# S5 input stage: products of the turned weights tied to the next half's transposes

## Chip, cores and metric

The kernel runs on one core of one Trainium2 chip. The metric is the time of one launch in device microseconds (us), the median of several runs. TensorE (PE) does matmuls and transposes, ScalarE (ACT) and VectorE (DVE) work element by element and empty PSUM, GpSimd (POOL) and SyncE (SP) here mostly issue DMAs. Each engine executes its own list of instructions in a fixed order; semaphores make one engine wait for another.

## The reference

One layer of an encoder, batch 1, 512 tokens, width 1024: a wide input projection feeds an S5 state-space branch and a gated MLP branch; both are merged by gates, followed by cross-attention to 256 memory tokens and a SwiGLU FFN. What matters here is the S5 branch:

```python
lam_bar = jnp.exp(lam * step)
b_bar = ((lam_bar - 1.0) / lam)[..., None] * b
bu = jnp.einsum('gpc,lbgc->lbgp', b_bar, u.astype(jnp.complex64))
...
_, states = lax.associative_scan(_linear_recurrence, (a, bu), axis=0, reverse=reverse)
...
return jnp.einsum('gcp,lbgp->lbgc', c, states).real
```

There are 32 groups of 16 channels with 64 complex states each, and two directions.

## The kernel before

The large projections run as three products of float32r halves (`whi`, `wlo`) for float32 accuracy. For each block of weights a DMA brings `wraw`, ScalarE casts it to `whi` (line 85), VectorE subtracts to get `wlo` (line 86), and TensorE multiplies (line 358; tiles `pt` in token form, `pf` in feature form). Their PSUM banks come from a pool of five. The S5 branch runs as side work in between: a Python generator (`s5_program`) emits its VectorE work when `tick` grants it time, and `later(n, fn)` puts a function that emits the next step some ticks ahead. A scheduler then sets the order on each engine from the program's dependencies and its own estimate of times, so that the order in which the code emits instructions is not the order of execution, except where `in_order` pins an instruction behind the one emitted just before it on its engine.

The scan works on chunks of 8 positions. The input stage `s5_inputs(o)` makes each chunk's contribution to the state, for four octets `o` of 8 groups and two halves `i` (real and imaginary part):

- VectorE forms the weights `e` in three steps of 128x1024 elements (lines 885, 887 and 889, into `wsx`; a slot of `wsx` is reused by the next octet's same half).
- `turn(i, e)` transposes them on TensorE, eight 128x128 transposes in two groups of four (line 864), each group into one PSUM bank `pw`; ScalarE copies each bank to `wt` (line 865).
- `apply(i, wt)` multiplies by `u`, eight products of 64 columns (line 871; two records each in the trace), into a bank `pz`; `keep` has ScalarE copy it into `zh` in two parts (lines 876 and 877).

The banks `pw` and `pz` come from the pool of three auxiliary banks, given out in the order in which the code asks for them: `aux` returns the next of the three, and the first instruction that writes it waits until the bank's last reader is done. `wt` has two buffers. When all eight halves are in `zh`, VectorE runs the scan (62 steps, from line 898), and the outputs follow much later (`py`, lines 922 to 924).

Around this stage the main stream runs the last part of the projection to `zv` (`pt`, emptied by the gelu of line 975) and the gate projection (`pf`, emptied by the sigmoid of line 1047). ScalarE also has the layer norm of `zt` here: centring (line 1008), squares (line 486) and scaling (line 1014, with the root from POOL, line 1013). Behind the stage come `mixing_setup` (`pws`, `pgb`, `prs`; lines 1027 to 1036) and the spatial mixing (`psv`, line 1063).

Of the kernel before, what the change touches and what calls it, by code (L numbers as in the profile page):

```python
# [41 lines left out]
NO = 4  # L42
GO = G // NO
# [9 lines left out]
def hybrid_layer_kernel(  # L53
# [8 lines left out]
    nc = tc.nc  # L62
# [14 lines left out]
    def bank(name):  # L77
        return pm.tile([P, 512], F32, tag="mm", name=name)

    def aux(name, shape=(P, 512)):  # L80
        return pa.tile(list(shape), F32, tag="aux", name=name)
# [11 lines left out]
    in_order = tc.keep_in_program_order  # L93
# [349 lines left out]
    def later(n, fn):  # L443

        side["later"].append((side["now"] + n, fn))
# [30 lines left out]
    ident = cp.tile([P, P], F32, name="ident")  # L476
# [139 lines left out]
    st = {}  # L616
# [150 lines left out]
    def inner(t, gs, n):  # L767

        return t[:, gs, :].unsqueeze(3).to_broadcast([P, GO, t.shape[2], n])

    def outer(t, gs, n):

        return t[:, gs, :].unsqueeze(2).to_broadcast([P, GO, n, t.shape[2]])

    def lc(t, g):
        return t[:, g].rearrange("p a b -> p (a b)")
# [72 lines left out]
    turned = set()  # L849

    def s5_inputs(o):

        gs = slice(o * GO, (o + 1) * GO)
        br, bi = st["b"]
        pr, pi = st["pw"]
        zh, u = st["zh"], st["u"]

        def turn(i, e):
            turned.add((o, i))
            wt = s5p.tile([P, GO, P], F32, tag="wt", name="wt", bufs=2)  # L860
            for hf in range(2):
                ps = aux("pw", (P, 4, P))
                for j in range(4):
                    nc.tensor.transpose(ps[:, j, :], lc(e, 4 * hf + j), ident)
                nc.scalar.copy(wt[:, 4 * hf:4 * hf + 4, :], ps)
            later(0.5, lambda: apply(i, wt))

        def apply(i, wt):
            ps = aux("pz", (P, GO, NCH))
            for g in range(GO):  # L870
                nc.tensor.matmul(ps[:, g, :], wt[:, g, :], u[:, o * GO + g, :], start=True, stop=True)  # L871
            zv = zh[:, :, i, gs].rearrange("p n g -> p g n")
            later(0.5, lambda: keep(zv, ps))

        def keep(zv, ps):
            nc.scalar.copy(zv[lo_], ps[lo_])
            nc.scalar.copy(zv[hi_], ps[hi_, :, ::-1])
            st["nz"] = st.get("nz", 0) + 1

        for i in range(2):  # L880
            while o > 0 and (o - 1, i) not in turned:
                yield None
            e = wsx[:, 2 + i].rearrange("p g (c l) -> p g c l", c=C)
            w = s5p.tile([P, GO, C, Q], F32, tag="etmp", name="etmp2")
            V.tensor_tensor(e, inner(br, gs, Q), outer((pr, pi)[i], gs, C), ALU.mult)
            yield 1.1
            V.tensor_tensor(w, inner(bi, gs, Q), outer((pi, pr)[i], gs, C), ALU.mult)
            yield 1.1
            V.tensor_tensor(e, e, w, (ALU.subtract, ALU.add)[i])
            yield 1.1  # L890
            later(1, lambda i=i, e=e: turn(i, e))
# [93 lines left out]
    u = s5p.tile([P, G, NCH], F32, tag="u", name="u")  # L985
# [74 lines left out]
    for h in range(H):  # L1060
        ps = bank("psv")
# [425 lines left out]
    for t0 in (0, 2):  # L1487
        ps = {t: bank(f"pt{t - t0}") for t in (t0, t0 + 1)}
# [77 lines left out]
    ps = [bank("pf0"), bank("pf1")]  # L1566
# [242 lines left out]
```

## Time and profile before

| | |
|---|---|
| median of 3 runs | 893.77 us (893.14 to 894.84) |
| span of the profiled execution | 891.3 us |
| the stage's transposes and products on TensorE | 83.2 to 151.7 us |
| TensorE busy in the span | 881.1 us |

The profile is of one execution, and the page gives its span (first to last instruction) but no launch time of its own; the runs' times include what lies before and after the span. A row of the chain of waits or of the order of time gives a start, a duration, the engine, the line and the tile written. In the order of time a bracket at the end is idle time of the engine before the row and what ended it. In the windows' answer each row is a stretch, then busy time and number of instructions of PE, its weight loads, DVE, ACT and POOL, the granted clock as a share of full speed, and the DMA load.

### The profile page before, as it was taken

Reading aid. Unit: us, or ns where it says so; the run is one execution under the profiler, and the core shown is the slowest. Engines: PE = TensorE matmul, PEld = TensorE weight load, DVE = VectorE, ACT = ScalarE, POOL = GpSimd, SP = SyncE. Lnnn points to the kernel's source line nnn. Section 1 sums busy time; section 2 is a strip of 40 time slices with the busy share of each in tenths; the row PEclk is TensorE's granted clock in tenths of the full one; section 3 lists DMA queues with packets and bytes.
Section 4 is the critical chain, followed back from the end, with each engine's and each line's share of the span. In section 5 each row is a group of like instructions: output and inputs, shape, how many; then the busy total and the mean of one; then the engine's idle time right before and its main releaser. Section 6 shows DMA issues by size and latency. Waiting matters only on the chain.

```text
span 891.3 us, 14796 instructions
## 1 busy us (share of the span) xinstructions
PE 881.1 (99%) x5744; PEld 788.0 (88%) x5744; DVE 642.5 (72%) x1048; ACT 487.4 (55%) x714; POOL 106.9 (12%) x165
## 2 busy tenths in 40 slices
PE   9999999999999999999999999999999999999996
PEld 6788888888889998889899978999999999988875
DVE  5697653889847368658856836676878777899875
ACT  5743994244396254347656534645555455655664
POOL 1005301111032111001001001101121111000010
PEclk9999999999999999999999999999999999999998
DMA  8667456978533789834579747627899999356672
GB/s 255 196 189 182 114 155 177 189 191 190 159 87 84 212 285 268 288 117 140 168 221 256 194 103 197 166 81 181 213 237 233 216 225 249 95 167 207 204 230 102
DMA packets 118408, 165.36 MB, mean 186 GB/s; under 512 B 11825, under 2 KB 84161, under 8 KB 118210
## 3 DMA queue, kind: packets, MB, share of 16 engines
q1 hardware_dynamic: 97474, 135.74, 47.9%
q0 software_dynamic: 20576, 28.15, 19.9%
q8 instruction: 45, 0.74, 0.3%
q10 hardware_dynamic: 288, 0.52, 0.2%
q14 instruction: 25, 0.20, 0.1%
HBM read 157.61 MB, written 46.63 MB: 229 GB/s over the span
## 4 chain that ended last, share of the span: by engine, by line
PE 97%; DMA 1%; SPq 1%; ACT 0%; DVE 0%; issue 0%; POOLq 0%; ACTq 0%
PE pf L358 26%; PE pt L358 17%; PE px L1110 12%; PE dx L358 6%; PE pq L1110 6%; PE dq L358 3%; PE pv L1110 3%; PE bx L1110 3%; PE qx L1110 2%; PE dv L358 2%; PE pz L871 2%; PE pk L814 2%; PE bq L1110 1%; PE qv L1110 1%; PE psc L358 1%; PE qq L1110 1%
## 5 line engine op out<-in xcount | busy, mean ns | idle before, releaser
L86 DVE TENSOR_TENSOR wlo<-wraw,whi 128x1024 fp32r<-128x1024 f32 (+1 forms) x145 | 172.2, 1189 | 101.2 <-ACT whi L85 101.0
L85 ACT CAST whi<-wraw 128x1024 fp32r<-128x1024 f32 (+1 forms) x145 | 148.6, 1026 | 152.2 <-PE pf L358 44.0
L358 PE MATMUL pf<-xn,whi 128*128 128x512 f32 x448 | 139.6, 391 | 0.0
L358 PEld LDWEIGHTS pf<-xn,whi 128*128 128x128 f32 x448 | 83.7, 188 | 17.0
L358 PE MATMUL pf<-xn,wlo 128*128 128x512 f32 x224 | 87.3, 390 | 0.0
L1110 PE MATMUL px<-fn,whi 128*128 128x256 f32 x480 | 83.4, 277 | 0.0
L1110 PEld LDWEIGHTS px<-fn,whi 128*128 128x128 f32 x480 | 72.7, 188 | 0.2
L85 ACT CAST whi<-b 128x1024 fp32r<-128x1024 f32 x40 | 42.2, 1055 | 50.4 <-PE px L1110 27.4
L86 DVE TENSOR_TENSOR wlo<-b,whi 128x1024 fp32r<-128x1024 f32 x40 | 48.9, 1223 | 27.0 <-ACT whi L85 27.0
L1110 PE MATMUL px<-fn,wlo 128*128 128x256 f32 x240 | 66.4, 277 | 0.0
L1110 PE MATMUL pq<-s,whi 128*128 128x256 f32 x320 | 55.0, 276 | 0.0
L358 PE MATMUL dx<-whi,s 128*128 128x512 f32 x170 | 53.4, 390 | 0.4 <-DVE h L1734 0.4
L85 ACT CAST whi<-t 128x1024 fp32r<-128x1024 f32 x30 | 31.6, 1054 | 35.6 <-PE pv L1110 12.4
L86 DVE TENSOR_TENSOR wlo<-t,whi 128x1024 fp32r<-128x1024 f32 x30 | 36.7, 1225 | 19.7 <-ACT whi L85 19.7
L358 PEld LDWEIGHTS pf<-xn,wlo 128*128 128x128 f32 x224 | 42.1, 188 | 8.7
L1110 PEld LDWEIGHTS pq<-s,whi 128*128 128x128 f32 x320 | 48.3, 188 | 0.0
L1110 PEld LDWEIGHTS px<-fn,wlo 128*128 128x128 f32 x240 | 45.1, 188 | 0.0
L358 PE MATMUL pt<-whi,xn 128*128 128x512 f32 x128 | 43.7, 412 | 0.7 <-ACT xn L85 0.7
L1110 PE MATMUL pq<-s,wlo 128*128 128x256 f32 x160 | 44.2, 276 | 0.0
L358 PEld LDWEIGHTS dx<-whi,s 128*128 128x128 f32 x170 | 31.8, 188 | 7.5 <-issue 0.8
L358 PE MATMUL dx<-wlo,s 128*128 128x512 f32 x85 | 33.0, 390 | 0.0
L275 POOL DMA_DIRECT2D dsum<-in_w_down_dram x12 | 13.3, 1105 | 162.4 <-DMA dsum<-in_w_down_dram 162.4
(453 smaller groups left out, 2296.8 us busy)
## 6 DMA issues: line engine op xcount, KB each, us to landing
wraw<-in_w_in_dram SPq DMA_DIRECT2D x36, 512.0 KB, 4.7
dsum<-in_w_down_dram SPq DMA_DIRECT2D x20, 512.0 KB, 5.4
wraw<-dsum SPq DMA_DIRECT2D x20, 512.0 KB, 4.1
b<-in_w_gate_dram SPq DMA_DIRECT2D x15, 512.0 KB, 5.4
b<-in_w_up_dram SPq DMA_DIRECT2D x15, 512.0 KB, 5.3
wraw<-in_w_down_dram SPq DMA_DIRECT2D x15, 512.0 KB, 4.4
dsum<-in_w_down_dram POOLq DMA_DIRECT2D x10, 512.0 KB, 8.1
dsum<-dsum POOLq DMA_DIRECT2D x10, 512.0 KB, 8.5
```

Of the source, the lines that this page charges most:

```text
L85: hi = nc.scalar.copy(dst_hi, src)
L86: lo = nc.vector.tensor_tensor(dst_lo, src, dst_hi.bitcast(F32), ALU.subtract)
L275: plan[j + step][1].append((0, lambda d=dst, x=more: nc.gpsimd.dma_start(d, x, accum_op=ALU.add)))
L358: m = nc.tensor.matmul(ps, a[x], b[y], start=start and i == 0, stop=stop and i == 2, skip_group_check=free)
L814: nc.tensor.matmul(ps[32 * j:32 * j + 32, q, :], bd[i][:, g].rearrange("p d c -> p (d c)"), lc(es[i], g), start=(i == 0), stop=False, tile ...
L871: nc.tensor.matmul(ps[:, g, :], wt[:, g, :], u[:, o * GO + g, :], start=True, stop=True)
L1110: nc.tensor.matmul(ps[:, j, :], a[x], b[y], start=start and j == k == i == 0, stop=k == 3 and i == 2, skip_group_check=True)
```

## The change

`turn` no longer schedules its own `apply`. It calls the `apply` of the half before right after emitting its own transposes and the copies out of them, and leaves its own products to the next `turn`; the last half's products are emitted by a call half a tick later. The transposes and the products are pinned in the order in which the code emits them.

```diff
             for hf in range(2):
                 ps = aux("pw", (P, 4, P))
                 for j in range(4):
-                    nc.tensor.transpose(ps[:, j, :], lc(e, 4 * hf + j), ident)
+                    in_order(nc.tensor.transpose(ps[:, j, :], lc(e, 4 * hf + j), ident))
                 nc.scalar.copy(wt[:, 4 * hf:4 * hf + 4, :], ps)
-            later(0.5, lambda: apply(i, wt))
+            apply_last()
+            st["turned"] = lambda: apply(i, wt)
+            if (o, i) == (NO - 1, 1):
+                later(0.5, apply_last)
+
+        def apply_last():
+            if "turned" in st:
+                st.pop("turned")()
 
         def apply(i, wt):
             ps = aux("pz", (P, GO, NCH))
             for g in range(GO):
-                nc.tensor.matmul(ps[:, g, :], wt[:, g, :], u[:, o * GO + g, :], start=True, stop=True)
+                in_order(nc.tensor.matmul(ps[:, g, :], wt[:, g, :], u[:, o * GO + g, :], start=True, stop=True))
             zv = zh[:, :, i, gs].rearrange("p n g -> p g n")
```

A pin only forbids an instruction to move ahead of the one emitted before it; the scheduler may still place other work in between. The order of TensorE's list in the two built programs, from the first turn to `psv` (`m` is a 128x512 matmul of the main stream, `pw` eight transposes, `pz` eight products, `pw/2` four transposes):

```
before: pw m23 pz m1 pw m23 pw pz m22 pz m3 pw m34 pz pw m20 pw pz m6 pz pw m23 pz pw
        m20 pws pgb m20 prs pz m45 psv
after:  pw m24 pw pz m15 pw m6 pz m27 pw pz m28 pw m3 pz m5 pw/2 m1 pw/2 m11 pz pw m20
        pz m4 pw m14 pz m10 pws m6 pgb m15 prs m1 pz m50 psv
```

Outside this stretch TensorE's order is the same. ScalarE's and VectorE's lists differ from the second octet on until the start of the scan, POOL's in the place of one DMA among four memsets, and SyncE's not at all. Counts of instructions are the same on every engine.

## Prediction

> **What bounds the kernel now.** I read the page's busy times and clock first, then TensorE's waits, then the chain of waits through the stage that the change touches, then ScalarE's order of time there.
>
> ```profile
> span 891.3 us, 14796 instructions
> PE 881.1 (99%) x5744; PEld 788.0 (88%) x5744; DVE 642.5 (72%) x1048; ACT 487.4 (55%) x714; POOL 106.9 (12%) x165
> PEclk9999999999999999999999999999999999999998
> PE 97%; DMA 1%; SPq 1%; ACT 0%; DVE 0%; issue 0%; POOLq 0%; ACTq 0%
> ...
> PE idle L556 <- DVE mhalf L481: 1.1, 1, 1.1
> PE pt L358 <- ACT ot_hi L85: 0.9, 2, 0.7
> PE pt L358 <- ACT xn L85: 0.7, 1, 0.7
> PE dx L358 <- DVE h L1734: 0.4, 1, 0.4
> ```
>
> TensorE is busy 99% of the span at full clock, and the last four rows are all its waits that the answer lists: 3.1 us, none of them in the S5 input stage. Any wait that the change creates in this stage is therefore new, and anything that TensorE loses has work queued behind it to the end. ScalarE's 55% is a mean over stages; the stage itself reads otherwise (us, then busy time and instructions of PE, PEld, DVE, ACT, POOL, clock, DMA):
>
> ```profile
> 89.33:120.23 30.90, 30.90 (x187) 27.22 (x186) 17.45 (x28) 30.70 (x49) 7.34 (x11) 1.00 0.40 106
> ...
> 89.33 1.15 ACT L1008 ACTIVATE zt<-zt,nm 128x1024 f32<-128x1024 f32 x1 [1.48 <-DVE nm L1006]
> ...
> 119.19 1.15 ACT L1014 ACTIVATE zt<-zt,r 128x1024 f32<-128x1024 f32 x1
> 120.23 1.08 ACT L876 COPY zh<-pz 64x512 f32<-64x512 f32 x1
> ```
>
> For 30.90 us ScalarE works 30.70: two engines are full at once, and TensorE escapes a wait only because what it takes from ScalarE was asked for early enough. That is the margin the change spends.
>
> **The change, part by part.** No instruction is added or removed on any engine; only places move, between 84 and 155 us of the profile. SyncE's queue and all its DMAs keep their order. POOL moves one accumulating DMA of `bsum` ahead of four memsets, on an engine that is busy 7.34 of the 30.90 us; VectorE reorders small layer-norm steps and S5 products at 17.45 of 30.90. I cost both at nothing; without that room, the POOL move costs the four memsets and the VectorE move one product, all ahead of work that TensorE takes later.
>
> *Islands on TensorE.* The stage's transposes, products, `pws` and `prs` stand as islands in the stream of 128x512 matmuls: 12 before, 17 after, by the two orders printed above.
>
> ```profile
> 84.24 5.24 PE pt L358 x23
> 89.49 1.73 PE pz L871 x16
> 91.22 0.29 PE pt L358
> ...
> 123.54 0.87 PE pw L864 x8
> ...
> 169.55 30.65 PE pf L358 x135
> ```
>
> In the undisturbed stream one matmul takes 30.65/135 = 0.227 us. The one behind a `pz` group takes 0.29, so leaving such a group costs 0.063; the 23 behind a `pw` group take 5.24 against 23 x 0.227 = 5.22, so leaving that costs 0.02. Islands that end in `pz` go from 5 to 7 (0.13), those that end in `pw` or a lone `pws` from 6 to 8 (0.04), and `prs` is now followed by a matmul instead of `pz` (0.06, as for `pz`). Sum +0.23, on the bound engine. From below: if all islands were free, 0; nothing here is a gain.
>
> *The sixth pair of transposes (o=2, i=1).* This is the main term. Auxiliary PSUM has three banks, given out in the program's order. The first `pw` bank of the sixth turn follows two `pw` and one `pz`, so it is the first bank of the fifth turn, free when ScalarE has copied that to `wt`. The pin sets these transposes behind 108 matmuls, four `pw` groups and four `pz` groups, counted from 84.24. TensorE gets there after 108 x 0.227 = 24.52, 4 x 0.87 = 3.48, 4 x 1.73 = 6.92, and leaving four `pz` and three `pw` islands 0.31: 35.23, so 119.47 by the chain, whose pieces are set about 0.16 behind the starts in the order of time (91.51 here, 91.35 there):
>
> ```profile
> 91.51 0.55 PE pw L864 x5
> ...
> 91.35 1.04 PE L864 MATMUL pw<-ident,wsx 128*128 128x128 f32 x8
> ```
>
> So TensorE is ready at 119.31. In the order before, this turn's transposes came at 123.38:
>
> ```profile
> 123.38 1.03 PE L864 MATMUL pw<-ident,wsx 128*128 128x128 f32 x8
> ...
> L865 ACT COPY wt<-pw x16: 565/588/609, 84.4 to 139.9; 128x512 f32<-128x512 f32 x16
> ```
>
> When is the bank free? In the new order ScalarE runs 38 instructions of the program from the activation at 89.33 up to the fifth turn's first copy. They are the same 38 by kind and number as stood between 89.33 and 120.23 before: three gelus, eight squares, four centrings, four scalings, four weight casts, six `wt` copies, three `zh` pairs, a table load with two sigmoids. The 30.70 us of work put the copy at 120.03 if ScalarE never idles, at 120.23 if it idles as before. With 0.588 for the copy it ends at 120.62 to 120.82. TensorE's start behind such a release is seen once:
>
> ```profile
> 523.89 0.59 ACT L85 CAST ot_hi<-po 128x512 fp32r<-128x512 f32 x1 [0.32 <-PE po L358]
> ...
> 524.53 0.50 PE L358 MATMUL pt<-whi,ot_hi 128*128 128x512 f32 x1 [0.68 <-ACT ot_hi L85]
> 524.87 0.40 PE L358 MATMUL pt<-wlo,ot_hi 128*128 128x512 f32 x1
> ```
>
> 0.05 us behind the cast's end, so 120.67 to 120.87 here: a wait of 1.36 to 1.56 us, of which I take 1.4, the end near no idling, because the new order puts other work between the layer-norm steps that follow from each other. The restart costs up to 0.34 - 0.227 = 0.11 more (524.53 to 524.87); I take 0.10, and 0 as the lower end. Queued behind the waiting transposes is the whole matmul stream: TensorE starts in order. The second half of the turn needs the second copy, half of "122.45 1.07" behind the first:
>
> ```profile
> 122.45 1.07 ACT L865 COPY wt<-pw 128x512 f32<-128x512 f32 x2
> ```
>
> about 0.5 us later, while four transposes (half of 0.87) and one matmul give TensorE 0.66: no second wait.
>
> *What is late next.* The scan starts after the last `zh` copy. The last `pz` now has 50 matmuls between itself and `psv` instead of 45, so it stands 5 x 0.227 = 1.1 us nearer the stage's start; with the stall the scan starts some 0.6 later, TensorE's stream 1.7 later. The scan gains room, and no wait on it follows.
>
> **Sum.** 1.4 + 0.10 + 0.23 = 1.73 us on a span of 891.3, so 893.0. The page gives the profiled execution its span alone; the median of the runs, 893.77, lies 2.5 above that, which I carry over: **895.5 us**, +0.19%. The forecast's own range runs from +1.2 (wait 1.1, no restart cost, islands 0.1) to +2.3 (wait 1.8, ScalarE idling 0.25 more than before): 895.0 to 896.1.
>
> **Rivals.**
>
> *Not slower: the loss is absorbed.* TensorE waits 0.9 us in two places for `ot_hi` and 0.4 for `h`, long after this stage. If these waits ended at times that the S5 stage does not move, they would take 1.3 of the 1.73 back: 894.2. It decides only if ScalarE and VectorE there are not themselves released by TensorE; the row at 523.89 says that they are ("<-PE po"). The other way to this result is an earlier copy: it must end by 119.3, 1.3 us before ScalarE's sum allows, and then only the islands remain: 894.0. Together 0.12.
>
> *The change doesn't do what it says.* By the built order only two of the eight product groups stand right behind transposes; the pins forbid moving up, and the scheduler still puts matmuls in between. Were all eight next to transposes with nothing between, the islands would be fewer than the 12 of before, and a gain would be bounded by the 0.4 us that all 12 cost (five times 0.063, six times 0.02). For faster by over 0.2%, 1.8 us, no row shows a source. 0.05, for what the profile does not tell: 891.8.
>
> *Slower by more: ScalarE falls further behind.* Every gap that ScalarE gets in the 38 instructions is added to TensorE's wait one for one. The tightest are the centrings, which wait for VectorE (1.48 us before the one at 89.33). One further gap of that size gives 1.73 + 1.48: 897.0. Against it: of 0.20 us of idling in the window there is little to repeat. 0.15.
>
> *The clock falls behind the wait.* After the 0.68 us wait the clock stayed whole:
>
> ```profile
> 523.40:525.40 2.00, 1.32 (x7) 0.77 (x6) 1.79 (x2) 0.76 (x2) 0.00 (x0) 1.00 0.00 0
> 525.40:529.00 3.60, 3.60 (x17) 2.86 (x16) 0.37 (x2) 0.59 (x1) 0.00 (x0) 1.00 0.81 274
> ```
>
> The wait here is twice as long. If the 3.60 us behind it ran at the 0.8 that the page's last slice shows, they would take 0.9 longer: 896.4. 0.03. The Trainium skill, "TensorE: Matmul & The Clock Gate", section "Part 1: The HAM clock gate (the "warmup" mystery)", states that the array's clock is halved after an idle window of about 3.4 us and comes back after as long a busy one; by that rule a wait of 1.4 us leaves the clock whole, though one halved window would cost an estimated 1.7 us. The trace agrees as far as its 0.68 us wait goes.
>
> **How the numbers follow.** What a measurement of this kernel can tell from no change is about 0.2%, 1.79 us or 895.56. My forecast of 1.73 lies almost on that bound. It holds 0.65: half of it on either side, 0.33 slower and 0.32 same. Not slower adds 0.12 to same; the further stall 0.15 and the clock 0.03 go to slower. Small chances rounded: slower 0.51, same 0.44, faster 0.05. The range reaches down past both not-slower cases to 893.8 and up past the further stall's 897.0 to 897.3; outside are the gain (0.05) and about 0.12 of the tails of these cases.
>
> **What would show it.** Right: TensorE's waits gain one row, `pw` L864 on ACT `wt` L865, 1.2 to 1.6 us, near 119.5 to 120.9; the copy that frees it starts at 120.0 to 120.3; groups L358, L864 and pz keep counts and mean durations; the first `psv` group comes 1.7 us later than here, and everything behind keeps that distance:
>
> ```profile
> 162.18 3.57 PE psv L1063 x32
> ```
> Wrong in the main term: no such wait, or one released by VectorE; wrong in what follows: the distance shrinks at the waits for `ot_hi` or `h`, or new waits of `py` on `ss` appear.

## The result, and the profile after

| | before | after |
|---|---|---|
| median | 893.62 us (892.41 to 895.77, 20 runs) | 894.70 us (893.99 to 898.56, 20 runs) |
| ratio after/before | | 1.0017, 95% interval 1.0009 to 1.0025 |
| span of the profiled execution | 891.3 us | 892.6 us |
| first transposes to first `psv` | 78.81 us | 80.19 us |

The changed kernel is slower by 0.17%, which is 1.5 us (0.8 to 2.2 by the interval). The ratio agrees with the quotient of the means; the medians differ by less, 1.1 us. The page of the kernel after: span, busy times, shares of the chain that ended last.

```profile
span 892.6 us, 14797 instructions
PE 881.8 (99%) x5744; PEld 788.1 (88%) x5744; DVE 642.5 (72%) x1048; ACT 486.7 (55%) x714; POOL 107.7 (12%) x165
PE 92%; ACT 3%; DMA 1%; issue 1%; DVE 1%; SPq 1%; POOL 0%; POOLq 0%; ACTq 0%
```

ScalarE's share of the chain has gone from 0% to 3%: somewhere TensorE now waits for it. The share is far more than the wait, because the chain runs back from there through some 31 us of ScalarE's queue (from 119.88 to 88.73). TensorE's waits in the kernel after (total, times, longest) say where.

```profile
...
PE pt L358 <- ACT ot_hi L85: 0.9, 2, 0.7
PE pw L864 <- ACT wt L865: 0.9, 1, 0.9
PE dx L358 <- DVE h L1741: 0.4, 1, 0.4
PE dx L358 <- DVE wlo L86: 0.4, 1, 0.4
```

The second row shown is new and is the one forecast. The old waits for `ot_hi` and `h` stand as they were; the last, for `wlo`, stands near the launch's end and comes and goes between profiles: the run without pins below, whose order is the same, has none. So does the wait for `xn` early in the launch: 0.7 before, none here, 1.6 without the pins. The order of time in the kernel after shows the place, first on TensorE, then on ScalarE.

```profile
82.61 1.04 PE L864 MATMUL pw<-ident,wsx 128*128 128x128 f32 x8
...
118.58 0.40 PE L358 MATMUL pf<-xn,wlo 128*128 128x512 f32 x1
119.88 0.66 PE L864 MATMUL pw<-ident,wsx 128*128 128x128 f32 x4 [0.90 <-ACT wt L865]
120.30 0.48 PE L358 MATMUL pf<-xn,whi 128*128 128x512 f32 x1
120.61 0.60 PE L864 MATMUL pw<-ident,wsx 128*128 128x128 f32 x4
...
162.80 3.40 PE L1070 MATMUL psv<-wsx,zt 128*128 128x128 f32 x29
...
88.73 1.15 ACT L1015 ACTIVATE zt<-zt,nm 128x1024 f32<-128x1024 f32 x1 [1.49 <-DVE nm L1013]
...
119.25 1.08 ACT L865 COPY wt<-pw 128x512 f32<-128x512 f32 x2
```

The matmul at 118.58 would be followed 0.227 us later, at 118.81. The first half of the sixth turn starts at 119.88, just as ScalarE has done the first of the fifth turn's two copies (119.25 and some 0.59). So the stop costs 1.07 us from start to start; the 0.90 in the bracket begins only at the end that the profile gives the matmul (118.98). Behind it nothing special follows: four transposes take 0.42 (119.88 to 120.30), about the 0.435 that half a group takes elsewhere, and the second half has no bracket.

The windows of the two kernels, before first (stretch, then us, busy time and count of PE, PEld, DVE, ACT, POOL, clock, DMA share, GB/s), give what the whole stage lost.

```profile
83.21:162.02 78.81, 78.81 (x447) 67.80 (x445) 43.93 (x90) 58.98 (x90) 16.75 (x32) 1.00 0.59 148
```

```profile
82.61:162.80 80.19, 79.29 (x447) 67.57 (x446) 43.54 (x89) 58.81 (x90) 17.59 (x32) 1.00 0.52 139
...
88.73:119.25 30.52, 30.25 (x182) 26.23 (x180) 16.14 (x27) 30.38 (x50) 8.17 (x11) 1.00 0.40 104
...
119.00:122.40 3.40, 2.52 (x15) 2.23 (x16) 3.37 (x3) 3.38 (x5) 0.00 (x0) 1.00 0.61 214
```

80.19 - 78.81 = 1.38 us more: 1.07 for the stop, 0.31 for the rest. Both ends of that stretch are the same instructions in every kernel below, and launch-to-launch differences ahead of the stage do not enter: the first transposes start at 83.21 in one profile and at 82.61 in the other, and up to 85.79 in the runs below, though TensorE's work ahead of them is the same. That is why I compare stretches of single profiles, and whole times only by many runs. Behind `psv` the two kernels have the same order on every engine; from the first `psv` to TensorE's end 722.42 us passed before and 722.92 after (0.4 of it the wait for `wlo`), so nothing of the loss comes back.

### The profile page after: what moved, and what is told of

The parts are those of the page before. It is cut to its first block, busy times and chain, and to the rows that moved or that the text cites. A ratio compares the mean times of both kernels' runs of the same rounds, so it can differ in the third digit from the quotient of the medians.

```text
span 892.6 us, 14797 instructions
## 1 busy us (share of the span) xinstructions
PE 881.8 (99%) x5744; PEld 788.1 (88%) x5744; DVE 642.5 (72%) x1048; ACT 486.7 (55%) x714; POOL 107.7 (12%) x165
## 4 chain that ended last, share of the span: by engine, by line
PE 92%; ACT 3%; DMA 1%; issue 1%; DVE 1%; SPq 1%; POOL 0%; POOLq 0%; ACTq 0%
PE pf L358 24%; PE pt L358 16%; PE px L1117 12%; PE dx L358 6%; PE pq L1117 6%; PE dq L358 3%; PE pv L1117 3%; PE bx L1117 3%; PE qx L1117 2%; PE dv L358 2%; PE pk L814 2%; PE bq L1117 1%; PE qv L1117 1%; PE psc L358 1%; PE qq L1117 1%; PE ptr L520 1%
```

## The experiments

Seven kernels ran beside the two, each 8 to 12 times. The stretch runs from the first transposes of the stage to the first `psv`, in one profile of each kernel; the medians of before are those of the same chip (31 and 29 runs).

| kernel | median, before there | ratio, 95% interval | stretch |
|---|---|---|---|
| after | 894.70, 893.62 | 1.0017, 1.0009 to 1.0025 | 80.19 |
| later emission without pins | 894.89, 893.96 | 1.0011, 0.9998 to 1.0023 | 80.18 |
| fifth turn's copies on VectorE | 897.00, 893.96 | 1.0036, 1.0021 to 1.0051 | 79.10 |
| all copies on VectorE | 893.91, 893.96 | 0.9994, 0.9983 to 1.0004 | 79.15 |
| before, more ScalarE work | 894.38, 893.96 | 1.0003, 0.9993 to 1.0014 | 79.15 |
| sixth turn in the main banks | 894.74, 893.88 | 1.0003, 0.9990 to 1.0016 | 79.84 |
| two scalings on VectorE | 894.13, 893.88 | 1.0000, 0.9988 to 1.0012 | 79.07 |
| after, more ScalarE work | 895.03, 893.88 | 1.0020, 1.0003 to 1.0037 | 80.69 |

### Which part of the change does it: the later emission without the pins

Against the kernel after, both pins go; the products are still emitted behind the next turn.

```diff
-                    in_order(nc.tensor.transpose(ps[:, j, :], lc(e, 4 * hf + j), ident))
+                    nc.tensor.transpose(ps[:, j, :], lc(e, 4 * hf + j), ident)
...
-                in_order(nc.tensor.matmul(ps[:, g, :], wt[:, g, :], u[:, o * GO + g, :], start=True, stop=True))
+                nc.tensor.matmul(ps[:, g, :], wt[:, g, :], u[:, o * GO + g, :], start=True, stop=True)
```

> The changed kernel with both pins taken away, so that only the later emission of the products is left. The built program's lists are then the same on every engine as with the pins. If the emission does all of the change: ratio 1.0010 to 1.0025, one wait of pw on wt of 0.8 to 1.0 us, and 80.0 to 80.4 us from the first pw to the first psv (78.81 before, 80.19 changed). If the pins matter: 78.8 to 79.2 us there and ratio 0.9993 to 1.0007.

Its waits have the row of the kernel after (`PE pw L864 <- ACT wt L865`: 0.9, once). Rows from its order of time:

```profile
84.29 1.03 PE L864 MATMUL pw<-ident,wsx 128*128 128x128 f32 x8
...
164.47 1.72 PE L1070 MATMUL psv<-wsx,zt 128*128 128x128 f32 x14
```

The same wait and the same stretch: 164.47 - 84.29 = 80.18 against 80.19. The built program has the order of the kernel after on every engine, and pins put alone into the kernel before leave its order as it was. The pins do nothing here; the place of the emission does everything. It does so in two ways. The pool hands out auxiliary banks in the order of the code: before, the fourth turn's products asked for a bank ahead of the fifth turn, so the sixth turn got *their* bank; after, they ask behind it, and the sixth turn gets the fifth turn's first bank. And the scheduler places the sixth turn sooner, behind 108 matmuls of the main stream instead of 126: it starts 119.88 - 82.61 = 37.27 us into the stage, the stop included, where it was 123.38 - 83.21 = 40.17. The whole time's interval reaches down to 0.9998, so the runs alone would not settle this; the stretch does.

### Is it ScalarE's copy: the fifth turn's two copies on VectorE

```diff
-                nc.scalar.copy(wt[:, 4 * hf:4 * hf + 4, :], ps)
+                (V.tensor_copy if (o, i) == (2, 0) else nc.scalar.copy)(wt[:, 4 * hf:4 * hf + 4, :], ps)
```

> The changed kernel, with the two copies of the fifth turn (o=2, i=0) from pw to wt made by VectorE, so that the sixth turn's bank no longer waits in ScalarE's queue. If the lost time is that wait: no wait of pw above 0.2 us, first pw to first psv 79.0 to 79.3 us (the islands' 0.2 to 0.4 us over 78.81 are left), ratio 1.0000 to 1.0008. If the islands or the later place of the products as such cost the time: 80.0 us or more, ratio 1.0010 to 1.0025.

In the stage it went as expected: no wait at a `pw` or `pz`, stretch 162.60 - 83.50 = 79.10. The whole time did not: 1.0036 instead of at most 1.0008. This kernel's order of time on TensorE, then its waits, then ScalarE's order of time:

```profile
83.50 1.03 PE L864 MATMUL pw<-ident,wsx 128*128 128x128 f32 x8
...
162.60 3.62 PE L1070 MATMUL psv<-wsx,zt 128*128 128x128 f32 x31
```

```profile
PE pf L358 <- ACT ya_hi L85: 1.1, 1, 1.1
PE pf L358 <- ACT yg_hi L85: 0.9, 1, 0.9
```

```profile
315.25 0.59 ACT L936 ACTIVATE y<-py 128x512 f32<-128x512 f32 x1
326.72 1.66 ACT L85 CAST yg_hi<-ygt 128x512 fp32r<-128x512 f32 x3 [1.32 <-DMA ygt<-yd]
```

The same rows in the kernel after:

```profile
312.23 0.60 ACT L936 ACTIVATE y<-py 128x512 f32<-128x512 f32 x1 [6.42 <-PE py L931]
322.82 0.63 ACT L85 CAST yg_hi<-ygt 128x512 fp32r<-128x512 f32 x1 [0.57 <-DMA ygt<-yd]
```

Two new waits, at 339.70 and 327.40, some 200 us behind the two copies. The scheduler, given another engine for two copies, also moved the S5 outputs later in its order: the last gelu of `y` starts at 315.25 rather than 312.23, and the cast to `yg_hi` at 326.72 rather than 322.82, held by the DMA of `ygt`. From the first `psv` to TensorE's end this kernel takes 725.77 us against 722.92, which is the miss: 2.0 of the 2.85 us are these two waits, and the rest was not traced. Why the scheduler moved that far work was not tried. As a test of the wait only the stretch can be read: without ScalarE's late copy the change costs 79.10 - 78.81 = 0.29 us.

### The same with an unchanged order behind the stage: all 16 copies on VectorE

```diff
-                nc.scalar.copy(wt[:, 4 * hf:4 * hf + 4, :], ps)
+                V.tensor_copy(wt[:, 4 * hf:4 * hf + 4, :], ps)
```

> The changed kernel, with all sixteen copies from pw to wt on VectorE, which takes 16 x 0.5 us off ScalarE. If ScalarE's lateness is the cause: no wait of pw or pz at all, 78.9 to 79.2 us from the first pw to the first psv, ratio 0.9998 to 1.0006. If not: 80.0 us or more. VectorE's own load rises by 16 x 0.6 us in 70; should that be the new bound, waits of pw on wsx (VectorE) appear instead.

The order of time on TensorE in this kernel:

```profile
83.00 1.04 PE L864 MATMUL pw<-ident,wsx 128*128 128x128 f32 x8
...
162.15 3.73 PE L1070 MATMUL psv<-wsx,zt 128*128 128x128 f32 x32
```

Stretch 79.15, no wait at a `pw` or `pz`, and behind `psv` the order of before (inside the stage TensorE's order is again a new one, with the sixth turn behind 103 matmuls); the whole time is that of before, 0.9994 (0.9983 to 1.0004). So the loss hangs on the wait for ScalarE. But this moves 16 copies, and ScalarE's whole queue gets shorter by them: it does not tell whether one late copy or ScalarE's load is the cause. The next runs change the load.

### ScalarE's load, taken away: two scalings on VectorE

The scalings of the layer norm for two of the four token tiles go from ScalarE to VectorE.

```diff
-        nc.scalar.activation(z, z, AF.Copy, scale=r)
+        if t in (2, 3):
+            nc.vector.tensor_scalar(z, z, r, None, ALU.mult)
+        else:
+            nc.scalar.activation(z, z, AF.Copy, scale=r)
```

> The changed kernel, with the layer norm's scaling of the last two token tiles on VectorE: 2.1 us less on ScalarE ahead of the fifth turn's copies, the S5 code as changed. If ScalarE's lateness is the cause: no wait of pw or pz, 79.0 to 79.3 us from the first pw to the first psv, ratio 1.0000 to 1.0008. If the new place of the products costs by itself: 80.0 us or more.

TensorE's order of time in this kernel:

```profile
84.67 1.03 PE L864 MATMUL pw<-ident,wsx 128*128 128x128 f32 x8
...
163.74 2.50 PE L1073 MATMUL psv<-wsx,zt 128*128 128x128 f32 x21
```

Stretch 79.07, no wait in the stage. The copies stay on ScalarE and the sixth turn takes the same bank. The fifth turn's first copy starts at 119.26, 34.59 us into the stage instead of 36.64: two activations less ahead of it are 2.05 us, more than the 1.07 by which it was late. TensorE is not later either: the sixth turn comes behind 106 matmuls, 35.75 us into the stage, where the kernel after was ready at 36.20. It is the load of ScalarE's queue: with 2 us to spare there the change costs 0.26 us in the stretch, and no stop.

### The load, added: one activation more, before and after

One activation of 128x1024 into scratch, behind the centring of the last token tile, in the kernel before and in the kernel after.

```diff
+        if t == NT - 1:
+            for _ in range(1):
+                nc.scalar.activation(squares[:, t, :], z, AF.Identity)
```

In the kernel before:

> The kernel before, with one activation of 128x1024 more on ScalarE (into a scratch that is overwritten; it computes nothing that is used), about 1.05 us, ahead of the fifth turn's copies; TensorE's order up to the seventh turn stays. Before, ScalarE released the sixth turn's first bank at 122.4, 0.9 us ahead of its transposes, and the second copy of wt at about 123.5, 0.7 us ahead of the products. If the margin on ScalarE is what the change spent: a new wait of pw or pz on ScalarE of 0.2 to 0.5 us in all, 79.0 to 79.5 us from the first pw to the first psv. If ScalarE had several us of room: no wait, 78.8 us.

Its order of time, first TensorE's, then ScalarE's:

```profile
85.79 0.93 PE L864 MATMUL pw<-ident,wsx 128*128 128x128 f32 x7
...
125.99 1.27 PE L864 MATMUL pw<-ident,wsx 128*128 128x128 f32 x8
127.09 1.99 PE L871 MATMUL pz<-u,wt 128*128 128x64 f32 x16
...
164.94 1.27 PE L1066 MATMUL psv<-wsx,zt 128*128 128x128 f32 x10
...
124.82 1.11 ACT L877 COPY zh<-pz 64x512 f32<-64x512 f32 x1
```

The sixth turn starts at 125.99, 0.06 behind the end of the copy of the fourth products (124.82 + 1.11): that is the bank it gets in the kernel before. There the copy ended at 122.43,

```profile
121.32 1.11 ACT L877 COPY zh<-pz 64x512 f32<-64x512 f32 x1
```

0.95 us ahead of the sixth turn at 123.38. The additional activation takes 1.06 us (0.96 to the next start) and uses that up, and the stretch grows by 0.34 to 79.15. TensorE's waiting list has no row for it: the group takes 1.27 instead of 1.03, and the products behind it 1.99 instead of 1.90. The list of its weight loads (PEld) has two, one for each half of the turn:

```profile
PEld pw L864 <- ACT zh L877: 0.3, 1, 0.3
...
PEld pw L864 <- ACT wt L865: 0.2, 1, 0.2
```

The kernel before was about one activation away from the same kind of stop.

In the kernel after:

> The changed kernel with the additional ScalarE activation of 128x1024 of e4. The scheduler answers by moving one scaling from ahead of the fifth turn's first copy to behind it, so the work ahead of that copy stays the same and the wait of the sixth turn stays at 0.8 to 1.0 us; zh of the fourth products comes 1.05 us later and should make the fifth products wait 0.3 to 0.5 us. 80.4 to 80.8 us from the first pw to the first psv, ratio 1.0013 to 1.0032. If TensorE's time there does not hang on ScalarE: 80.0 to 80.3 us as changed.

Its order of time on TensorE and on ScalarE:

```profile
82.43 1.03 PE L864 MATMUL pw<-ident,wsx 128*128 128x128 f32 x8
...
119.75 0.66 PE L864 MATMUL pw<-ident,wsx 128*128 128x128 f32 x4 [0.94 <-ACT wt L865]
...
123.29 2.00 PE L878 MATMUL pz<-u,wt 128*128 128x64 f32 x16
...
163.12 3.06 PE L1073 MATMUL psv<-wsx,zt 128*128 128x128 f32 x26
...
119.11 0.59 ACT L865 COPY wt<-pw 128x512 f32<-128x512 f32 x1
119.57 1.17 ACT L1024 ACTIVATE zt<-zt,r 128x1024 f32<-128x1024 f32 x1
```

80.69, 0.50 more than after and not the 1.05 that the activation takes: the scheduler put a scaling of 1.17 us behind the fifth turn's first copy, so that this copy is no later than it was. What is late instead is the copy of the fourth products, as expected. The fifth products (123.29) start 0.05 behind its end, and the weight loads name it:

```profile
PEld pz L878 <- ACT zh L884: 0.4, 1, 0.4
```

The same activation costs 0.34 before and 0.50 after.

### The bank: the sixth turn in the main stream's banks

```diff
-                ps = aux("pw", (P, 4, P))
+                ps = bank("pw").rearrange("p (a b) -> p a b", a=4) if (o, i) == (2, 1) else aux("pw", (P, 4, P))
```

> The changed kernel, with the sixth turn's two pw banks taken from the main pool of five, so that its transposes wait for no copy of the fifth turn. The scheduler then sets the sixth turn right behind the fourth products, and the fifth turn and these products 4 matmuls (0.9 us) earlier; the fourth products' bank is that of the third, which ScalarE has copied to zh at about 115.0 in the changed kernel's profile, while TensorE is ready at about 114.3. If ScalarE's lateness is the cause, the wait only moves: pz on zh, 0.5 to 0.9 us, 79.7 to 80.1 us from the first pw to the first psv, ratio 1.0004 to 1.0018. If the rotation of the auxiliary banks alone made it: no wait, 79.0 to 79.3 us, ratio 1.0000 to 1.0008.

Its order of time on TensorE, then on ScalarE:

```profile
84.53 1.04 PE L864 MATMUL pw<-ident,wsx 128*128 128x128 f32 x8
...
116.94 2.00 PE L878 MATMUL pz<-u,wt 128*128 128x64 f32 x16 [0.58 <-ACT zh L884]
118.78 1.04 PE L864 MATMUL pw<-ident,wsx 128*128 128x128 f32 x8
...
164.37 1.83 PE L1070 MATMUL psv<-wsx,zt 128*128 128x128 f32 x15
...
115.87 1.02 ACT L884 COPY zh<-pz 64x512 f32<-64x512 f32 x1
```

The sixth turn (118.78) now waits for nothing and comes 3.0 us earlier in the stage than in the kernel after. But the products of the fourth turn (116.94) moved up as well, behind the fifth turn, and run into the next late copy: they start 0.05 behind the end of the copy of the third products (115.87 + 1.02). The stretch is 79.84, only 0.35 less than after. Another bank moves the wait to the next reader in ScalarE's queue; less work on ScalarE removes it. The whole time, 1.0003 (0.9990 to 1.0016), lies just below the expected range and can't be told from before, nor from the +1.03 us that the stretch shows.

## Why the prediction was right, and where it was not

*What bounds, and the loss being kept.* Right. TensorE's stop in this stage had work behind it to the end: 1.38 us in the stretch, 1.5 by the ratio, and no shorter way behind `psv`. The waits for `ot_hi` and `h` stayed at 0.9 and 0.4, so the rival in which they absorb the loss is false. The total lies in the forecast's range, but below its middle.

*The main term.* Place, tile, lines and releaser were right: the first half of the sixth turn on the fifth turn's first copy, and no wait of the second half. The size was not: 1.4 + 0.10 forecast, 1.07 measured, just under the 1.1 at which the range began; the row shows 0.9, not the 1.2 to 1.6 that I named as the sign. Three parts of it can be told. TensorE got to the bank at 118.81, 36.20 us into the stage, 0.10 later than the computed 119.31 (36.10 into it). ScalarE's run from the activation at 88.73 to the copy took 30.52 us, 0.18 less than the 30.70 that I took as its lower end; the activation itself stood 6.12 us into the stage in both kernels. And TensorE lost nothing at the restart, where I had 0.10 and allowed 0. 1.36 - 0.10 - 0.18 = 1.08, and that is the wait. The wait is a small difference of two sums of 30 us and more, and 0.18 is 0.6% of ScalarE's. My range from 30.70 to 30.90 allowed only for idling and took the 30.70 us of work as fixed, and that is the term that was mis-sized: in the new order the same 38 instructions are 30.38 us of work, with 0.14 idle. This is the order and not scatter, for the kernel without pins takes 30.51 (90.41 to 120.92). Of the 0.38 us less than before from start to start, 0.24 is at two places: before, what followed the cast at 112.59 and the copy at 115.39 started only at their ends, 1.07 and 0.58 us behind their starts, where behind the other casts and copies of these two stretches the next one starts after 0.93 to 0.95 and 0.46 to 0.49.

*The islands.* 0.23 forecast, 0.31 beside the stop in the kernel after: near, a little low. That the number of islands makes it is not shown. The three kernels that keep the later emission and have no stop show 0.29, 0.34 and 0.26 (79.10, 79.15 and 79.07 against 78.81), though the same prices would give 0.23, 0.17 and 0.17: their orders have 17, 14 and 14 islands.

*What makes the order.* This step failed. I wrote that "the pin sets these transposes behind 108 matmuls" and that "the pins forbid moving up". The run without pins has the same order, wait and stretch. The order comes from the later emission, through the bank's turn in the pool and through the scheduler, which placed the sixth turn 2.9 us sooner in the stage. The time came out all the same because I took the places from the built order and not from the reason.

*What is late next.* The scan's first step starts at 154.1 before and at 153.7 after. From the stage's first transposes that is 70.9 us before and 71.1 after: 0.2 later, not 0.6, since the stop was 0.43 shorter than forecast. No wait on it followed.

*Costed at nothing.* The moves on POOL and VectorE: no new wait of TensorE in the stage names either. Right as far as the waits show.

*The other rivals.* ScalarE did not fall further behind (30.52 us, not 30.90 and more). The clock stayed whole around the stop: 1.00 from 119.00 to 122.40. Its price there was misread, though: the 0.8 of the page's last slice is a mean of 17.4 us at 1.00 and 4.8 us at 0.50 (from 886.50 on). A stretch of 3.41 us at 0.50, as other kernels show it below, would cost an estimated 1.7 us, not 0.9. That the change doesn't do what it says is half true, since the pins do nothing, but no gain came of it.

## What to carry to other kernels

Where a pool hands out buffers in the order of the code, emitting a step later also changes whose reader frees the next step's buffer: list for each buffer the last reader in the new rotation and how late the engine of that reader runs. An engine with 55% of the span can be full for 30 us; a tensor engine that has no wait beside it may have only one activation of margin, and a stage's loss is best read between two of its own instructions, not from the whole time. Take a change of several parts apart before naming the part that acts: here the part in its name did nothing.

## What the runs showed of the hardware that was not expected

The granted clock can halve behind a short stop. In the kernel with all copies on VectorE, TensorE waited 1.7 us early in the launch:

```profile
3.92:7.33 3.41, 1.99 (x5) 0.66 (x4) 0.93 (x3) 1.80 (x5) 0.55 (x1) 1.00 0.89 266
7.33:10.74 3.41, 3.13 (x11) 2.69 (x12) 2.87 (x6) 3.20 (x6) 0.00 (x0) 0.50 1.02 398
```

and in the kernel before with more ScalarE work there was a wait of 1.79 us that ended at 17.69:

```profile
14.93:18.34 3.41, 1.56 (x10) 1.02 (x9) 2.07 (x6) 1.94 (x6) 0.00 (x0) 1.00 0.63 112
18.34:21.76 3.42, 3.42 (x10) 2.64 (x9) 2.32 (x8) 1.01 (x4) 1.10 (x2) 0.50 0.93 235
```

The clock is 0.50 for one stretch of 3.41 us and whole again in the next. In these traces it changes only at multiples of 3.413 us from one another: in the last kernel at 8.10, 11.52, 18.34, 21.76 and 892.15. So a stop has to be read against these borders. TensorE was busy 1.99 and 1.56 of the 3.41 us ahead of the halving. Busy time alone does not decide it, as a stretch with the whole stop of the kernel without pins, and the end of the launch in the kernel before with more ScalarE work, show:

```profile
119.57:122.98 3.41, 2.52 (x16) 1.87 (x15) 2.38 (x3) 3.40 (x7) 0.00 (x0) 1.00 0.38 142
```

```profile
885.33:888.74 3.41, 2.06 (x18) 1.85 (x16) 1.91 (x7) 1.99 (x7) 0.56 (x1) 1.00 0.01 2
888.74:892.15 3.41, 0.00 (x0) 0.00 (x0) 1.36 (x2) 1.09 (x2) 0.92 (x1) 1.00 0.63 239
```

Here 2.52 and 2.06 us busy kept the clock whole in the next stretch, while in the same kernel 2.10 (4.69 to 8.10) did not. The Trainium skill, "TensorE: Matmul & The Clock Gate", section "Part 1: The HAM clock gate (the "warmup" mystery)", says that the clock is halved after at least one idle window of about 3.4 us. The length of the window agrees with these rows; that the window must be idle does not, if idle means without work, for one with TensorE busy 1.99 of 3.41 us was enough. The stop that was forecast, 1.50 us instead of 1.07, would have left an estimated 2.52 - 0.43 = 2.09 us busy in that stretch of the kernel without pins, among values that went either way: the rival of the clock was nearer than the chance of 0.03, which I took from a wait of 0.68 us, made it. In the kernel after, the stop fell across a border at 119.44 and left 2.95 and 2.98 us busy on its two sides, so where the borders fall counts too. What decides beside the busy time was not measured.
